# The v projection of the first stage in units of 512 channels, with tokens as the stationary side

## The chip, the cores and the metric

The kernel runs on one core of one Trainium2 chip. Its time is the device time of one execution in microseconds (us). The engines of the core are called PE (TensorE, matmuls; PEld are its weight loads), DVE (VectorE), ACT (ScalarE), POOL (GpSimd) and SP (SyncE, which issues most DMAs). Three executions of the kernel before took 2548.44, 2550.02 and 2554.36 us; the median is 2550.02 us.

## The reference

The kernel computes one layer of an encoder on 1280 tokens (1024 of a prompt, 256 of a sample) with a model width of 2048. The part that matters here is the combined input projection:

```
hn   = rmsnorm(x, norm_w)                      # 1280 x 2048
proj = einsum('btd,dp->btp', hn, w_in)         # 2048 -> 4*1024 + 5*1024 + 16 columns
na_q, na_k, na_v, na_g, ml_qk, ml_v, ml_o, ml_z, ml_gp = split(proj, ...)
```

Then neighbourhood attention uses na_q, na_k and na_v (8 heads of 128 channels), a bidirectional mLSTM uses ml_qk after a convolution, and ml_v (4 heads of 256 channels); gates, an output projection and a last rmsnorm follow. "v" below means na_v and ml_v together: 2048 columns of w_in, 16 blocks of 128 channels. All is float32; the kernel reaches the accuracy with three matmul passes over a high and a low part of both operands (high x high, high x low, low x high).

## The kernel before, in words

**Stages.** The tokens are cut in two groups. The first stage projects the first 768 tokens (GA, two halves of 384) for all columns; the second stage projects the remaining 512 tokens (among others proj_v, line 738), and attention, mLSTM and the output projection follow. Only the first stage's order is touched by the change.

**The first stage.** `pair_a` (line 479) makes two blocks of 128 channels, a "pair", at a time; a pair is named by its first block (A56 is blocks 56 and 57). The contraction over 2048 and the 768 tokens and 256 channels are each halved, and the product of the 2 x 2 blocks is made by a seven-product scheme (Strassen's, in Winograd's form): sums of quarters of x are ready in SBUF (tiles xb and xg), sums of quarters of the weights are made for each pair, and the seven products are added up into four results. The products run in the order 1, 5, 6, 4, 7, 2, 3 within each of four steps r. In each step two contraction blocks kk of 128 are done. A matmul is 128x384: the weights stand, 384 tokens move (`mm_c`, line 286, three passes). One pair has 7 x 8 x 3 = 168 of them.

**Who feeds whom.** SP loads 512 KB of weights for each r (tile ra, three buffers, line 526). POOL makes four sums of weights in each r (tile wt, line 531). ACT and DVE split every operand into a high and a low part (`split_a`, lines 184 and 185; tile wsa, eight buffers, so a split can be at most eight ahead of PE). In the last r the seven products are folded into four results: ACT copies the first (line 498), DVE adds the others from PSUM (line 494) and scales (line 263, `out_scaled`). PSUM has eight banks, three of tag "pr" and five of tag "a"; a pair takes three and four. DVE works strictly in its own order.

**What follows a pair** is a generator (`finish_a`) that the next pair advances a little after some products: for convolution pairs (blocks 24 to 39) it holds the taps (lines 424 and 430, tile cv) and stores; for q and k it splits and stores; for v pairs (from block NCH = 56) it transposes the results on PE to have tokens in rows (line 470, six couples of transposes), and `store_v` (line 233) splits and stores them: for the first four groups of 256 channels (the attention's v) two DMAs of 64 rows for each token tile (line 247), for the others one DMA (line 243). Output tiles are vo (one buffer) and pc (five buffers, shared with the results).

**The order of the work** is a list: A4, A6, then for i in 0 to 7 a convolution pair QK0 + 2i, a v pair NCH + 2i, and two other pairs. So the cycle i = 0 is A24, A56, A8, A10, and i = 1 is A26, A58, A12, A14. The sums of weights of the pairs A24, A32 and A8 to A22 are also stored for the second stage (tensor sD, line 547, by SP). A scheduler places the instructions on each engine by its own estimate of times; the code is not simply run in the order in which it is written.

## Time and profile before

| what | value |
| --- | --- |
| median of three executions | 2550.02 us |
| the profiled execution | 2548.95 us, span 2547.2 us |
| granted TensorE clock | 0.999 |
| first stage, pairs A24 to A52 | 150.15 to 1066.52 us, four pairs in some 118 us |
| one v pair without what follows it (A56) | 180.64 to 209.76 us |
| the pair behind it (A8) | 209.76 to 240.13 us |

The span runs from the first to the last instruction. A row of a list of stretches gives, for one stretch of time, how long each engine was busy, with its number of instructions in brackets, then the granted clock, the busy share of the DMA engines and GB/s. A row of the timeline gives start and length in us, engine, source line, operation, output and inputs, shape and number. In a row of one tile the three numbers are the shortest, the median and the longest duration in ns (of landings, in us from a DMA's issue).

### The profile page before, as it was taken

What the parts mean: (1) busy time and instruction counts of PE and PEld (TensorE: products, weight loads), DVE (VectorE), ACT (ScalarE), POOL (GpSimd) and SP (SyncE); (2) the same over time, 40 slices, a digit from 0 to 9 for tenths busy, and PEclk for the clock granted to TensorE, in tenths of its full rate; (3) what the DMA queues carried; (4) which work ended last, traced back from release to release, by engine and by line L of the source; (5) the groups of instructions that cost most, each with busy time, mean ns of one, the idle gap of its engine ahead of it and who ended that gap; (6) DMA issues with size and microseconds to landing.
All of it is one profiled execution on the core that took longest, in us unless ns stands there. A gap on an engine that the chain in (4) does not pass through costs nothing.

```text
span 2547.2 us, 44753 instructions
## 1 busy us (share of the span) xinstructions
PE 2527.0 (99%) x15126; PEld 2366.8 (93%) x15126; DVE 1978.3 (78%) x4040; ACT 1349.3 (53%) x3051; POOL 591.4 (23%) x894
## 2 busy tenths in 40 slices
PE   8999999999999999999999999999999999999998
PEld 8999999999999999999999899899898888888886
DVE  8768888898969798988875676776875665889695
ACT  8635545444444444475655665666665653344445
POOL 0434545444444444510000011010100103000001
PEclk9999999999999999999999999999999999999999
DMA  6556474636433343476778888888877849646227
GB/s 216 159 160 206 137 233 132 182 120 192 130 115 128 108 129 100 133 246 210 232 248 270 268 267 288 276 260 272 299 223 242 286 129 356 199 149 211 88 87 256
DMA packets 307757, 505.67 MB, mean 199 GB/s; under 512 B 48992, under 2 KB 195080, under 8 KB 307528
## 3 DMA queue, kind: packets, MB, share of 16 engines
q1 hardware_dynamic: 304568, 491.01, 60.2%
q0 software_dynamic: 2960, 11.80, 1.2%
q8 instruction: 120, 1.97, 0.3%
q14 instruction: 109, 0.89, 0.1%
HBM read 374.18 MB, written 128.52 MB: 197 GB/s over the span
## 4 chain that ended last, share of the span: by engine, by line
PE 83%; DMA 2%; DVE 1%; ACT 1%; issue 0%; SPq 0%; ACTq 0%; POOLq 0%; POOL 0%
PE po L1654 15%; PE pc L686 15%; PE pv L769 5%; PE A16b L286 1%; PE A52b L286 1%; PE A44b L286 1%; PE A40b L286 1%; PE A20b L286 1%; PE A48b L286 1%; PE A50b L286 1%; PE A42b L286 1%; PE A18b L286 1%; PE A14b L286 1%; PE A54b L286 1%; PE A70b L286 1%; PE A68b L286 1%
## 5 line engine op out<-in xcount | busy, mean ns | idle before, releaser
L1654 PE MATMUL po<-wo,mo 128*128 128x512 f32 x1620 | 375.6, 393 | 0.0
L1654 PEld LDWEIGHTS po<-wo,mo 128*128 128x128 f32 x1620 | 304.1, 188 | 70.5
L178 DVE TENSOR_TENSOR ws<-wr,ws 128x512 fp32r<-128x512 f32 x144 | 98.5, 693 | 40.0 <-ACT ws L177 39.5
L177 ACT CAST ws<-wr 128x512 fp32r<-128x512 f32 x144 | 87.6, 617 | 67.7 <-PE pc L686 55.5
L177 ACT CAST mo<-mb 128x640 fp32r<-128x640 f32 x72 | 52.0, 726 | 110.6 <-PE po L1654 100.1
L118 POOL TENSOR_SCALAR rs<-rs 128x1 f32<-128x1 f32 x10 | 4.4, 440 | 373.6 <-DVE rs L1628 373.4
L178 DVE TENSOR_TENSOR mo<-mb,mo 128x640 fp32r<-128x640 f32 x72 | 59.0, 825 | 31.3 <-ACT mo L177 31.3
L1597 DVE TENSOR_TENSOR y<-y,po 128x512 f32<-128x512 f32 x90 | 58.0, 684 | 13.2 <-PE po L1654 13.0
L177 ACT CAST mo<-ms 128x640 fp32r<-128x640 f32 x40 | 28.9, 725 | 50.7 <-PE po L1654 32.6
L178 DVE TENSOR_TENSOR wsv<-wr_v,wsv 128x512 fp32r<-128x512 f32 x64 | 44.6, 702 | 14.1 <-ACT wsv L177 13.9
L177 ACT CAST wsv<-wr_v 128x512 fp32r<-128x512 f32 x64 | 38.9, 617 | 24.5 <-PE pv L769 13.0
L424 DVE SCALAR_TENSOR_TENSOR pcv<-pco,cw_sb,pcv 128x516 f32<-128x516 f32 x48 | 36.5, 760 | 8.5 <-ACT pcv L418 8.5
L1611 ACT ACTIVATE jk<-y 128x512 f32<-128x512 f32 x40 | 25.2, 630 | 29.8 <-DVE y L1597 29.5
L178 DVE TENSOR_TENSOR mo<-ms,mo 128x640 fp32r<-128x640 f32 x40 | 32.9, 823 | 9.8 <-ACT mo L177 9.8
L131 ACT ACTIVATE xq<-xq 128x1024 f32<-128x1024 f32 x20 | 21.2, 1060 | 34.3 <-DMA xq<-in_xtok_dram 32.0
L1110 POOL MEMSET mls_0v<- 128x2 f32 x4 | 0.4, 102 | 162.5 <-DVE S_dt.float L178 137.1
L286 PE MATMUL fb<-xg,fw 128*128 128x384 f32 x192 | 34.6, 334 | 0.0
L286 PEld LDWEIGHTS fb<-xg,fw 128*128 128x128 f32 x192 | 33.4, 188 | 0.0
L807 DVE CUSTOM_DVE_ANT_0 nap_0st<-nap_0s,nap_0bt 128x384 f32<-128x384 f32 x32 | 17.7, 553 | 19.8 <-PE nap_0s L802 7.8
L1560 DVE TENSOR_TENSOR ms<-mb,mb 128x640 f32<-128x640 f32 x40 | 32.9, 823 | 0.0
L263 DVE TENSOR_TENSOR pco<-pc,rstdb 128x512 f32<-128x512 f32 x28 | 19.1, 687 | 16.7 <-PE pc L686 15.8
L810 ACT ACTIVATE nap_0st<-nap_0st,nap_0sm 128x384 f32<-128x384 f32 x32 | 19.8, 617 | 21.9 <-DVE nap_0sm L807 21.9
(2770 smaller groups left out, 8507.5 us busy)
## 6 DMA issues: line engine op xcount, KB each, us to landing
wr<-in_w_in_dram SPq DMA_DIRECT2D x72, 512.0 KB, 4.9
wr_v<-in_w_in_dram SPq DMA_DIRECT2D x32, 512.0 KB, 5.0
wb<-in_w_o_dram SPq DMA_DIRECT2D x48, 256.0 KB, 3.4
xq<-in_xtok_dram SPq DMA_DIRECT2D x20, 512.0 KB, 4.1
mb<-mx POOLq DMA_DIRECT2D x32, 320.0 KB, 7.9
y<-in_xtok_dram SPq DMA_DIRECT2D x35, 256.0 KB, 5.3
wr_wp<-in_w_o_dram SPq DMA_DIRECT2D x16, 512.0 KB, 6.5
vS<-vo SPq DMA_DIRECT2D x24, 256.0 KB, 5.2
```

Of the source, the lines that this page charges most:

```text
L131: S.activation(raw, raw, AF.Square, accum_out=ssq[g][:, t, q : q + 1])
L177: S.copy(hi, src)
L178: return V.tensor_tensor(lo, src, f(hi), op=ALU.subtract)
L286: PE.matmul(o, w(a_), x(b_), start=first and m == 0, stop=last and m == 2)
L424: V.scalar_tensor_tensor(dst[:, a:n], src[:, a + j - pad : n + j - pad], cw_sb[:, ct, j : j + 1], dst[:, a:n], op0=ALU.mult, op1=ALU.add,)
L686: PE.matmul(pb[j], t[j][:, wi, c : c + P], xs[xi], start=first and m == 0, stop=last and m == 2,)
L769: PE.matmul(outs[tt], xs[:, tt * P : (tt + 1) * P], t[:, wi, q * w : (q + 1) * w], start=first and m == 0 and (gates or tt % 2 == 0), stop ...
L810: S.activation(st, st, AF.Exp, bias=sm[:, 0:1], scale=-1.0, accum_out=sm[:, 2:3])
L1560: V.tensor_tensor(t, x, y_, op=op)
L1597: V.tensor_tensor(Y[p, q, tt], Y[p, q, tt], bk, op=op)
L1611: S.activation(jk, Y[p, q, tt], AF.Square, accum_out=ss[t][:, c : c + 1])
L1654: PE.matmul(bk[tt], m[xi][:, tt * P : (tt + 1) * P], w[wi], start=first and kk == 0 and j == 0, stop=last and j == 2, skip_group_check=True,)
```

## The change

**Units of 512 channels.** v is no longer made in eight pairs but in four units V0, V2, V4 and V6 of 512 channels (`unit_v`), which stand in the even cycles only: A24, V0, A8, A10, then A26, A12, A14, and so on. In a unit the tokens stand (slices of 128 of the tiles xb and xg) and the weights move, 256 wide, so that the result has tokens in rows at once and no transposes are needed. The seven-product scheme halves the 768 tokens (three slices of 128 each), the contraction and the 512 channels. A unit has 7 x 8 x 3 slices x 3 passes = 504 matmuls of 128x256.

**Two passes.** Seven products of 384 x 256 would take ten and a half banks of PSUM. Products 1, 5, 6, 7 and 3 are made in a first pass over the eight kk, and 2 and 4 in a second, which reads the half of the weights that it needs again. Two products share a bank for the third slice (h0, h1, h3). The first pass loads 512 KB in two DMAs for each kk, the second 512 KB in two DMAs for each r: 24 DMAs of weights in a unit, where two pairs had 8.

**Folds and stores.** ACT copies product 1, and DVE's `plus` adds the others in pieces of 512 and 256 columns. C1 and C3 are ready after the first pass, and their six token tiles are stored during the second (`finish_v`); C0 and C2 are completed by products 4 and 2 and stored during the next pair. The scaling by the norm is done in `store_v` for each token (lines 180 and 181 with a scale), no longer by `out_scaled`. The host lays the columns of v out anew, and proj_v's split follows that.

**Order on PE.** Here is the start of the first v pair, before. A56b5 is the bank of product 5, A56s05 the split operand of step 0 and product 5.

```order
L286 MATMUL A56b1_2169<-xb0_242,A56s01_2178 128x384 x3
L286 MATMUL A56b1_2169<-xb1_246,A56s01_2178 128x384 x3
L286 MATMUL A56b5_2170<-xg1_0_244,A56s05_2189 128x384 x3
L286 MATMUL A56b5_2170<-xg1_1_248,A56s05_2189 128x384 x3
L286 MATMUL A56b4_2172<-xg2_0_245,A56s04_2213 128x384 x3
L286 MATMUL A56b4_2172<-xg2_1_249,A56s04_2213 128x384 x3
```

The same place on PE after the change, in V0: V0b1 holds two slices of product 1, V0h0 the third.

```order
L481 MATMUL V0b1_2171<-V0s01_2180,xb0_242 128x256 x6
L481 MATMUL V0h0_2169<-V0s01_2180,xb0_242 128x256 x3
L481 MATMUL V0b5_2172<-V0s05_2194,xg1_0_244 128x256 x6
L481 MATMUL V0h1_2170<-V0s05_2194,xg1_0_244 128x256 x3
L481 MATMUL V0h0_2169<-V0s06_2212,xg1_0_244 128x256
L481 MATMUL V0b6_2173<-V0s06_2212,xg1_0_244 128x256 x6
```

One split operand now serves nine matmuls of 256 columns in place of six of 384, and the operands have changed sides.

**Order on DVE at the start of A8.** Before, the folds of A56 (A56c) stood there between the splits of A8 and the end of A24's convolution:

```order
L185 TENSOR_TENSOR A8s04_2552<-A8r0_2517,A8s04_2552 128x256
L185 TENSOR_TENSOR A8s07_2564<-A8t07_2561,A8s07_2564 128x256
L494 TENSOR_TENSOR A56c1_2417<-A56c0_2416,A56b7_2173 128x384
L185 TENSOR_TENSOR A8s02_2573<-A8r0_2517,A8s02_2573 128x256
L494 TENSOR_TENSOR A56c1_2417<-A56c1_2417,A56b5_2170 128x384
L494 TENSOR_TENSOR A56c0_2416<-A56c0_2416,A56b5_2170 128x384
L494 TENSOR_TENSOR A56c0_2416<-A56c0_2416,A56b2_2174 128x384
L181 SCALAR_TENSOR_TENSOR A24c1_2079<-A24cv1_2326,A24ch1_2505 128x766
L494 TENSOR_TENSOR A56c1_2417<-A56c1_2417,A56b4_2172 128x384
```

After, V0o3 and V0o5 are output tiles of V0 in the one buffer of vo, and V0c0 and V0c2 take the products of the second pass:

```order
L181 SCALAR_TENSOR_TENSOR V0o3_2858<-V0c1_2748,rstdc0_229,V0o3_2858 128x2x128
L185 TENSOR_TENSOR A8s06_3068<-A8t06_3065,A8s06_3068 128x256
L185 TENSOR_TENSOR A8s04_3077<-A8r0_3037,A8s04_3077 128x256
L185 TENSOR_TENSOR A8s07_3094<-A8t07_3091,A8s07_3094 128x256
L185 TENSOR_TENSOR A8s02_3103<-A8r0_3037,A8s02_3103 128x256
L491 TENSOR_TENSOR V0c0_2717<-V0c0_2717,V0b2_2790 128x512
L181 SCALAR_TENSOR_TENSOR V0o5_2895<-V0c1_2748,rstdc0_229,V0o5_2895 128x2x128
L185 TENSOR_TENSOR A8s03_3120<-A8t03_3117,A8s03_3120 128x256
L491 TENSOR_TENSOR V0c2_2765<-V0c2_2765,V0b4_2791 128x512
L491 TENSOR_TENSOR V0c2_2765<-V0c2_2765,V0h3_2789 128x256
```

The output V0o5 stands ahead of the fold of V0b4, and A8's product 6 is given the bank of V0b4.

**Order on DVE in an odd cycle.** Before, the convolution of A26 stood among the splits of the v pair A58:

```order
L185 TENSOR_TENSOR A58s17_3708<-A58t17_3706,A58s17_3708 128x256
L424 SCALAR_TENSOR_TENSOR A26cv0_3600<-A26c0_3480,cw_sb_961,A26cv0_3600 128x764
L185 TENSOR_TENSOR A58s12_3717<-A58r1_3656,A58s12_3717 128x256
L185 TENSOR_TENSOR A58s13_3732<-A58t13_3730,A58s13_3732 128x256
L424 SCALAR_TENSOR_TENSOR A26cv0_3600<-A26c0_3480,cw_sb_961,A26cv0_3600 128x765
```

After, it stands in the same rhythm among the splits of A12:

```order
L185 TENSOR_TENSOR A12s17_4217<-A12t17_4214,A12s17_4217 128x256
L424 SCALAR_TENSOR_TENSOR A26cv0_4103<-A26c0_3982,cw_sb_961,A26cv0_4103 128x764
L185 TENSOR_TENSOR A12s12_4226<-A12r1_4162,A12s12_4226 128x256
L185 TENSOR_TENSOR A12s13_4242<-A12t13_4239,A12s13_4242 128x256
L424 SCALAR_TENSOR_TENSOR A26cv0_4103<-A26c0_3982,cw_sb_961,A26cv0_4103 128x765
```

The convolution has moved from a v pair into a pair whose sums are also stored. Behind the first stage the order on all engines is what it was.

The diff:

```diff
--- before.py
+++ after.py
@@ -434,8 +434,6 @@
     def finish_a(n1, Cn):
         nm = f"A{n1}"
         for j in range(2):
-            if n1 >= NCH:
-                break
             if QK0 <= n1 < OT0:
                 ct = n1 - QK0 + j
                 DM.dma_start(qb[ct], Cn[j][:, GA - 4 :])
@@ -460,21 +458,119 @@
                     V.scalar_tensor_tensor(Cn[j], th, 1.0, Cn[j], op0=ALU.add, op1=ALU.mult)
                 DM.dma_start(pT[n1 + j][:, 0:GA], Cn[j])
             yield
-        if n1 >= NCH:
+    def finish_v(u, z, C):
+        for tt in range(3):
+            t = 3 * z + tt
+            if tt == 1:
+                vo = wa.tile([P, GA], F32R, tag="pc", name=f"V{u}o{t}", bufs=NPC)
+                vo = vo[:, :512].rearrange("p (a d) -> p a d", a=2)
+            else:
+                vo = wa.tile([P, 2, 256], F32R, tag="vo", name=f"V{u}o{t}", bufs=1)
+            store_v(u, t * P, vo, C[:, tt * 256 : (tt + 1) * 256], rcs[0][:, t : t + 1])
             yield
-            yield
-            yield
-            for tt in range(GA // P):
-                b = bank("a", f"{nm}v{tt}")
-                for j in range(2):
-                    PE.transpose(b[:, j * P : (j + 1) * P], Cn[j][:, tt * P : (tt + 1) * P], ident)
-                if tt in (1, 3):
-                    vo = wa.tile([P, GA], F32R, tag="pc", name=f"{nm}vo{tt}", bufs=NPC)
-                    vo = vo[:, :512].rearrange("p (a d) -> p a d", a=2)
-                else:
-                    vo = wa.tile([P, 2, 256], F32R, tag="vo", name=f"{nm}vo{tt}", bufs=1)
-                store_v((n1 - NCH) // 2, tt * P, vo, b[:, :256])
-                yield
+
+    def unit_v(u, bg):
+        nm = f"V{u}"
+        C = {}
+
+        def mm_v(b, i, kk, t, first, last):
+            for tt in range(3):
+                o = b[i][0][:, tt * 256 : (tt + 1) * 256] if tt < 2 else b[i][1]
+                own = tt == 0 or tt == 2 and b[i][2]
+                for m, (xi, wi) in enumerate(((0, 0), (0, 1), (1, 0))):
+                    PE.matmul(
+                        o, xop(i, kk, xi)[:, tt * P : (tt + 1) * P], t[:, wi],
+                        start=first and own and m == 0, stop=last and m == 2 and (tt == 1 or tt == 2 and b[i][3]),
+                    )
+
+        def parts(c, b):
+            return ((c[:, 512:], b[1]), (c[:, :512], b[0]))
+
+        def plus(q, src, bi, halves=(0, 1)):
+            for z in halves:
+                V.tensor_tensor(
+                    parts(C[q], bi)[z][0], parts(C[src], bi)[z][0], parts(C[src], bi)[z][1],
+                    op=ALU.add,
+                )
+
+        b = {}
+        h = [bank("a", f"{nm}h{j}") for j in range(2)]
+        b[1] = bank("pr", f"{nm}b1"), h[0][:, :256], True, False
+        b[5] = bank("pr", f"{nm}b5"), h[1][:, :256], True, False
+        b[6] = bank("pr", f"{nm}b6"), h[0][:, 256:], False, True
+        b[7] = bank("a", f"{nm}b7"), h[1][:, 256:], False, True
+        b[3] = bank("a", f"{nm}b3"), bank("a", f"{nm}h2")[:, :256], True, True
+        for kk in range(8):
+            r, q = divmod(kk, 2)
+            raw = wa.tile([P, 1024], F32, tag="ra", name=f"{nm}r{kk}", bufs=NRA)
+            for j in range(2):
+                DM.dma_start(
+                    raw[:, j * 512 : (j + 1) * 512].rearrange("p (f c) -> p f c", f=2),
+                    w_in[NCH // 2 + u + j, r].rearrange("p (f q c) -> p f q c", f=2, q=2)[:, :, q],
+                )
+            A = {(j, f_): raw[:, (2 * j + f_) * 256 :][:, :256] for j in range(2) for f_ in range(2)}
+
+            def summed(i, x, y_, op):
+                t = wa.tile([P, 256], F32, tag="wt", name=f"{nm}t{kk}{i}", bufs=NWT)
+                G.tensor_tensor(t, x, y_, op=op)
+                return t
+
+            src = {1: A[0, 0]}
+            for i in (1, 5, 6, 7, 3):
+                if i == 5:
+                    src[5] = summed(5, A[1, 0], A[1, 1], ALU.add)
+                elif i == 6:
+                    src[6] = summed(6, src[5], A[0, 0], ALU.subtract)
+                elif i == 7:
+                    src[7] = summed(7, A[0, 0], A[1, 0], ALU.subtract)
+                elif i == 3:
+                    src[3] = summed(3, A[0, 1], src[6], ALU.subtract)
+                t = wsa(f"{nm}s{kk}{i}")
+                split_a(t[:, 0], t[:, 1], src[i])
+                mm_v(b, i, kk, t, kk == 0, kk == 7)
+                if kk < 7:
+                    if i in (5, 7):
+                        next(bg, None)
+                    continue
+                if i == 1:
+                    for _ in bg:
+                        pass
+                    C[0] = pc(f"{nm}c0")
+                    S.copy(C[0][:, :512], b[1][0])
+                elif i == 6:
+                    S.copy(C[0][:, 512:], b[1][1])
+                    C[1] = pc(f"{nm}c1")
+                    plus(1, 0, b[6])
+                elif i == 7:
+                    C[2] = pc(f"{nm}c2")
+                    plus(2, 1, b[7])
+                    C[3] = pc(f"{nm}c3")
+                    plus(3, 2, b[5])
+                    plus(1, 1, b[5])
+                elif i == 3:
+                    plus(1, 1, b[3])
+        bg = chain(finish_v(u + 1, 1, C[3]), finish_v(u, 1, C[1]))
+        h = bank("a", f"{nm}h3")
+        b[2] = bank("pr", f"{nm}b2"), h[:, :256], True, False
+        b[4] = bank("pr", f"{nm}b4"), h[:, 256:], False, True
+        for r in range(4):
+            raw = wa.tile([P, 1024], F32, tag="ra", name=f"{nm}q{r}", bufs=NRA)
+            for j in range(2):
+                DM.dma_start(raw[:, j * 512 : (j + 1) * 512], w_in[NCH // 2 + u + j, r][:, 512:])
+            for q in range(2):
+                kk = 2 * r + q
+                for i, j in ((2, 0), (4, 1)):
+                    t = wsa(f"{nm}s{kk}{i}")
+                    split_a(t[:, 0], t[:, 1], raw[:, j * 512 + q * 256 :][:, :256])
+                    mm_v(b, i, kk, t, kk == 0, kk == 7)
+                    next(bg, None)
+                    if kk == 7:
+                        plus(j * 2, j * 2, b[i], (0, 1) if j else (1,))
+            if r == 3:
+                plus(0, 0, b[2], (0,))
+        for _ in bg:
+            pass
+        return chain(finish_v(u, 0, C[0]), finish_v(u + 1, 0, C[2]))
 
     def pair_a(n1, bg=iter(()), hook=None, first=False, pinned=False):
         nm = f"A{n1}"
@@ -615,7 +711,7 @@
     order = [4, 6]
     rest = list(range(KT0, QK0, 2)) + list(range(OT0, NCH, 2))
     for i in range(NU):
-        order += [QK0 + 2 * i, NCH + 2 * i, *rest[2 * i : 2 * i + 2]]
+        order += [QK0 + 2 * i, *((NCH + 2 * i,) if i % 2 == 0 else ()), *rest[2 * i : 2 * i + 2]]
     pools = []
 
     def second_pools():
@@ -625,7 +721,10 @@
 
     bg = opening
     for i, n1 in enumerate(order):
-        bg = pair_a(n1, bg, second_pools if i == len(order) - 1 else None, i == 0, i == 1)
+        if n1 >= NCH:
+            bg = unit_v((n1 - NCH) // 2, bg)
+        else:
+            bg = pair_a(n1, bg, second_pools if i == len(order) - 1 else None, i == 0, i == 1)
         if i == 1:
             gates_a()
         k = i - 4
@@ -746,7 +845,7 @@
             outs = [pb[t // 2][:, (t % 2) * 256 : (t % 2) * 256 + 256] for t in range(nt)]
         for r in range(4):
             raw = w_piece(w_in[NCH // 2 + u, r], f"v{u}_{r}")
-            rawv = raw.rearrange("p (j f q c) -> p f q j c", j=2, f=2, q=2)
+            rawv = raw.rearrange("p (f q c) -> p f q c", f=2, q=2)
             if gates:
                 graw = wb.tile([P, 2, 2, 16], F32, tag="wgr", name=f"wg{r}", bufs=2)
                 DM.dma_start(
@@ -755,10 +854,7 @@
             for f_ in range(2):
                 t = wb.tile([P, 2, 544], F32R, tag="wsp", name=f"wsv_{u}_{r}_{f_}", bufs=4)
                 t4 = t[:, :, : 2 * w].rearrange("p h (k c) -> p h k c", k=2)
-                h2, l2 = (
-                    t4[:, z, :, 0:256].rearrange("p q (j c) -> p q j c", j=2) for z in range(2)
-                )
-                split(h2, l2, rawv[:, f_])
+                split(t4[:, 0, :, 0:256], t4[:, 1, :, 0:256], rawv[:, f_])
                 if gates:
                     split(t4[:, 0, :, 256:272], t4[:, 1, :, 256:272], graw[:, f_])
                 for tt in range(nt):
@@ -1756,6 +1852,8 @@
     w_in = np.ascontiguousarray(
         ch.reshape(2, 4, 2, P, nb // 2, 2, P).transpose(4, 1, 3, 5, 0, 2, 6).reshape(nb // 2, 4, P, 1024)
     )
+    vw = w_in[NCH // 2 :].reshape(NU, 4, P, 2, 2, 2, P).transpose(0, 1, 2, 4, 5, 3, 6)
+    w_in[NCH // 2 :] = vw.reshape(NU, 4, P, 1024)
     gorder = [d * 8 + w_ * 4 + h for w_ in range(2) for d in range(2) for h in range(4)]
     w_g = np.ascontiguousarray(
         cols["gp"][:, gorder].reshape(KT, P, 16).transpose(1, 0, 2).reshape(P, KT * 16)
```

## The prediction

> **What bounds the kernel now.** I read the page's busy times first, then the chain that ended last, then stretches of the first stage (the only stage whose order the change touches), then the timeline inside one v pair.
>
> ```profile
> span 2547.2 us, 44753 instructions
> PE 2527.0 (99%) x15126; PEld 2366.8 (93%) x15126; DVE 1978.3 (78%) x4040; ACT 1349.3 (53%) x3051; POOL 591.4 (23%) x894
> PE 83%; DMA 2%; DVE 1%; ACT 1%; issue 0%; SPq 0%; ACTq 0%; POOLq 0%; POOL 0%
> ```
>
> PE works 99% of the span and the chain runs through it. Busy alone would not prove it, since matmul ends are modelled, so here are the stretches of one v pair (A56), the pair behind it (A8) and the next (A10), then seven stretches of three pairs each, first and sum:
>
> ```profile
> core 0: us, PE busy (x) PEld busy (x) DVE busy (x) ACT busy (x) POOL busy (x), PEclk, DMA share, GB/s
> 180.64:209.76 29.12, 29.12 (x169) 29.12 (x169) 28.83 (x46) 15.19 (x35) 15.04 (x15) 1.00 0.41 119
> 209.76:240.13 30.37, 30.37 (x179) 30.10 (x179) 24.92 (x51) 13.99 (x38) 14.45 (x18) 1.00 0.70 217
> 240.13:269.50 29.37, 29.37 (x172) 29.33 (x172) 22.86 (x46) 14.86 (x36) 15.09 (x16) 1.00 0.67 216
> ...
> 180.64:269.48 88.84, 88.84 (x518) 88.53 (x518) 76.59 (x141) 44.03 (x107) 44.59 (x48) 1.00 0.60 184
> ...
> sum 622.49, PE 622.29 PEld 620.30 DVE 540.24 ACT 301.22 POOL 301.45; mean PE 88.90 PEld 88.61 DVE 77.18 ACT 43.03 POOL 43.06
> ```
>
> The granted clock is 1.00 and in these stretches PE has no idle time. So in the first stage time is the number of matmuls times the spacing of their starts. But DVE is busy 28.83 of 29.12 us in the v pair that also carries the convolution of the pair before it: there is a second engine close behind.
>
> ```profile
> 180.64 1.20 PE L286 MATMUL A56b<-xb,A56s 128*128 128x384 f32 x6
> 181.67 6.40 PE L286 MATMUL A56b<-xg,A56s 128*128 128x384 f32 x36
> 187.91 1.20 PE L286 MATMUL A56b<-xb,A56s 128*128 128x384 f32 x6
> ...
> 208.72 1.20 PE L286 MATMUL A56b<-xg,A56s 128*128 128x384 f32 x6
> ...
> 219.12 0.38 PE L470 MATMUL A56v<-ident,A56c 128*128 128x128 f32 x2
> ```
>
> The 36 start between 181.67 and 187.91: 6.24 us, 173.3 ns each; 168 of them are the 29.12 us.
>
> **The change part by part.**
>
> Removed matmuls: eight v pairs of 168, 8 x 29.12 = 233.0 us. Removed transposes with all that they upset: the seven stretches last 622.49 us, 21 pairs at 29.12 would be 611.5; the 11.0 us over, times 8/7, is 12.5 us.
>
> Added: four units of 504 matmuls of 128x256, 2016. The nearest rows are proj_v's, the same form (tokens stationary, w_in moving, three passes); I show the row that opens a run of 27 starts and the row behind it, then matmuls with another moving operand that step faster, and twelve starts of proj_v's wider form:
>
> ```profile
> 1096.11 0.29 PE L769 MATMUL pv<-wsv,x_0l 128*128 128x272 f32 x1
> ...
> 1097.61 0.29 PE L769 MATMUL pv<-wsv,x_0l 128*128 128x272 f32 x1
> ...
> 1119.87 0.52 PE L769 MATMUL pv<-wsv,x_0h 128*128 128x256 f32 x3
> ...
> 1123.06 0.40 PE L769 MATMUL pv<-wsv,x_9h 128*128 128x256 f32 x2
> ...
> 1365.94 2.43 PE L1408 MATMUL S14by<-xs,S14s 128*128 128x256 f32 x20
> 1368.20 0.40 PE L769 MATMUL pv<-wsv,x_0h 128*128 128x256 f32 x2
> ...
> L769 PEld LDWEIGHTS pv<-wsv,x_0h x64: 187/188/192, 1095.7 to 1835.5; 128*128 128x128 f32 x64
> ```
>
> 3.19 us / 27 = 118.1 ns; the x20 give 2.26 / 20 = 113.0 ns. the wider form 1.50 / 12 = 125 ns. I take 118.1, since the new operands are of that form, and keep the other two as ends: 2016 x 0.1181 = 238.1 us (227.8 to 252.0). The stationary side is loaded anew for every matmul, and a load lasts 188 ns, more than the spacing; loads plainly overlap with work here. The Trainium skill, "TensorE: Matmul & The Clock Gate", section "The mechanism", says that weight loads overlap matmuls in flight only when the row group differs, and section "LDWEIGHTS (loading the stationary operand)" gives columns / 1.2, an estimate of 107 ns for 128; by that, an estimate, the 672 loads that are added would cost 72 us and the change would lose. All loads here use the same 128 rows, and the trace's 118.1 ns disagrees, so the sum goes by the trace.
>
> Matmuls and transposes together: 238.1 - 233.0 - 12.5 = -7.4 us. The saving is small because more, shorter matmuls cost almost what is saved.
>
> Weights are split into as many tiles as before (56 for two pairs, 56 for a unit) and summed as often (32). Three things on DVE and POOL lie closer together than before, and here PE may have to wait:
>
> ```profile
> 173.99 0.59 DVE L185 TENSOR_TENSOR A56s<-A56r,A56s 128x256 fp32r<-128x256 f32 x1 [0.56 <-ACT A56s L184]
> ...
> 184.76 0.55 DVE L263 TENSOR_TENSOR A24c<-A24c,rstdb 128x384 f32<-128x384 f32 x1
> 185.23 0.96 DVE L185 TENSOR_TENSOR A56s<-A56t,A56s 128x256 fp32r<-128x256 f32 x1
> 186.11 0.41 DVE L185 TENSOR_TENSOR A56s<-A56r,A56s 128x256 fp32r<-128x256 f32 x1
> 187.32 1.00 DVE L424 SCALAR_TENSOR_TENSOR A24cv<-A24c,cw_sb,A24cv 128x764 f32<-128x764 f32 x1
> ...
> 206.17 0.41 DVE L185 TENSOR_TENSOR A56s<-A56t,A56s 128x256 fp32r<-128x256 f32 x1
> ...
> 208.92 0.54 DVE L494 TENSOR_TENSOR A56c<-A56c,A56b 128x384 f32<-128x384 f32 x1
> ...
> 216.61 0.41 DVE L185 TENSOR_TENSOR A8s<-A8r,A8s 128x256 fp32r<-128x256 f32 x1
> ...
> 217.04 1.20 PE L286 MATMUL A8b<-xb,A8s 128*128 128x384 f32 x6
> ...
> L531 POOL TENSOR_TENSOR A56t<-A56r x8: 737/800/1440, 168.3 to 195.7; 128x256 f32<-128x256 f32 x8
> ```
>
> First pass with convolution. The first split of A56 is done at 174.58, 6.1 us before PE needs it (180.64); the last at 206.58, 2.1 us before 208.72. DVE lost 4.0 us of lead in 29.12 us. Its work there, alone: 28 splits x 0.41, ten convolution steps x 1.0, seven folds x 0.54, four scalings x 0.55 = 27.5 us; it took 33.1, so each of POOL's 16 sums cost it about 0.35 us (a split takes 0.96 instead of 0.41 when it meets one, at most 0.55). In the new unit the convolution is over after six of eight steps: 30 splits, twelve convolution steps, the same folds and scalings, 30.3 us, and 24 sums at 0.35, in all 38.7 against 30 x 9 x 0.1181 = 31.9 us of PE. The 6.8 us over meet a lead of 6.1: PE would wait 0.7 us per unit, 2.8 in four; if DVE's idle moments count for part of the 0.35, nothing. Ends 0 and, at 0.55, 5.5 us per unit. I take 0.35 per unit, 1.4 us. POOL itself has four sums per 5.3 us; at its longest, 1.44 us, they would not fit, at 0.8 easily.
>
> Start of the next pair. The unit's outputs leave through tile vo, which has one buffer; each waits for the store before it.
>
> ```profile
> L247 SPq DMA_DIRECT2D vS<-A56vo x12: 451/484/1287, 224.2 to 246.1; - x12
> L177 ACT CAST A56vo<-A56v x6: 363/372/375, 220.1 to 244.7; 128x256 fp32r<-128x256 f32 x6
> L178 DVE TENSOR_TENSOR A56vo<-A56v,A56vo x6: 409/410/425, 223.1 to 245.1; 128x256 fp32r<-128x256 f32 x6
> ...
> DMA to landing us min/median/max: 2.5/4.1/5.3
> ...
> DMA to landing us min/median/max: 2.1/2.2/2.3
> ```
>
> (The last line is A64vo's, one store per tile in place of two.) In DVE's order of the new A8, V0o5 stands ahead of the folds of V0b4, and A8's product 6 needs that bank; behind V0o5 stand A8's own splits too. From the end T of the unit's last product 6, PE has two products of the first pass, 16 of the second (18 x 1.06 us) and 25 matmuls of A8: it needs the bank at T + 23.5. DVE is done with the first output about T + 6.0 (folds of 3072 columns at 0.54 per 384, four operations of 0.41); three trips of the buffer (0.37 + 0.41 + about 1.0 for two issues + 4.1 = 5.9) end at T + 23.7, and a split (0.41) and a fold of 768 columns (1.1) follow: T + 25.2, 1.7 us late. At a landing of 2.5 us nothing is late. I take 1 us for A8 and 1 for A16. A40 and A48 have a trip of 3.3 us and no wait. The boundary of the two passes costs nothing: product 4 takes the bank whose fold is among the first after T, and PE comes there 3 us after T.
>
> Odd cycles. Units exist only in every other cycle, so the convolutions of A26, A30, A34 and A38 go into A12, A20, A44 and A52, and their lag meets folds in the pair behind. Before, that place was A8: its eighth split ended at 217.02, PE began on it at 217.04, no wait but nothing to spare. A14 and A22 have, besides, splits of q and k. Ends 0 and 1.5 us each; I take 0.75, so 1.5 us.
>
> Covered: second reading of half the weights. 8 x 512 KB in the first pass, one per 5.3 us (before: per 7.3), and 4 x 512 KB in the second, with three buffers (over 10 us ahead) against landings of 3.6 us at a DMA share of 0.41:
>
> ```profile
> L526 SPq DMA_DIRECT2D A56r<-in_w_in_dram x4: 333/358/384, 158.0 to 179.8; - x4
> ...
> DMA to landing us min/median/max: 3.6/3.6/3.7
> ```
>
> 24 issues instead of 8 on SP, 16 x 0.36 = 5.7 us more per unit of 59.5 us, ahead of stores of v that are late anyway. If pieces of 1 KB made the landing three times as long, the cover would go. ACT (15.19 of 29.12 us) loses nothing that matters.
>
> Sum: -7.4 + 1.4 + 2 + 1.5 = -2.5 us. The profiled execution took 2548.95 us (span 2547.2), so 2546.5; the median of the runs, 2550.0, is 1.1 above it: 2547.6.
>
> **Rivals.** Faster: PE never waits, and steps are shorter. No wait gives -7.4, 2542.6; at 113.0 ns, 10.3 less, 2532.3. For it: waits are small guesses; against: all L769 rows of this form step at 118.
>
> Slower, DVE against POOL in the first pass: it decides above 0.32 us of loss per sum (24 x 0.32 = 31.9 + 6.1 - 30.3), and 0.35 was worked out. At 0.45, 3.1 us per unit, 12.4 in all, 2558.6; at 0.55, 22 us, 2568. Against: DVE idles at places in A56. The Trainium skill, "SBUF — State Buffer", section "SBUF: two separate sides", says that a DVE operation with two SBUF inputs and a GpSimd operation exclude each other for a whole instruction; that is the 0.96 for 0.41 and speaks for the upper end here.
>
> Slower, stores: if v's stores land at 5.3 us, the trip is 7.1, the bank is free at T + 28.8 and A8 and A16 each wait 5.3 us: 8.6 more than the 2 taken, 2556.2. It decides from a landing of 3.5 us.
>
> Slower, loads: if weight loads of 188 ns set the step, 2016 x 0.070 = 141 us more, near 2689. Only L769 speaks against it, strongly.
>
> **Numbers.** Sum's case 0.43 (its own range 2542 to 2554), faster rival 0.17, DVE against POOL 0.21, stores 0.16, loads 0.03. Below 0.2% (5.1 us) a measurement of this kernel can't tell a change from none. Faster: 0.10 of the sum's case, 0.15 of the first rival. Slower: 0.03, 0.16 of DVE against POOL, 0.10 of stores, 0.03 of loads. Same is the rest, 0.43. The range, 2537 to 2566, leaves out the shorter steps, the uppermost part of DVE against POOL and the loads, less than 0.2.
>
> **What would show it.** In the changed trace: v matmuls at 118 ns; V0's first pass 42.5 us, second 17.0, any excess with PE waiting on A-split or V0s by DVE; a PE wait in A8 and A16 released by a V0c fold; A14 and A22 within 1 us of 29.4; no transposes. Wrong by much if one of the waits recurs at every split.

## The result and the profile after

The changed kernel takes 2554.85 us (median of 21 executions, 2552.10 to 2558.54), the kernel before 2550.84 us (21 executions beside them, 2548.44 to 2555.22). The ratio is 1.0017, 95% interval 1.0011 to 1.0023: slower by a little, 2.8 to 5.9 us. I had forecast 2547.6 us, slightly faster. The time lies within the range, but on the other side of no change. The prediction also held that below 0.2% a change can't be told from none; with 21 executions of each kernel this one, of 0.17%, can.

Busy times and the chain of the changed kernel:

```profile
span 2551.1 us, 45919 instructions
PE 2527.2 (99%) x15702; PEld 2363.9 (93%) x15702; DVE 1966.4 (77%) x4008; ACT 1343.9 (53%) x3051; POOL 608.1 (24%) x894
PE 75%; DVE 6%; DMA 3%; issue 1%; ACT 1%; SPq 0%; ACTq 0%; POOLq 0%; POOL 0%; DVEq 0%
```

PE is as busy as before, and 99% again hides the matter. The chain tells it: DVE holds 6% of it where it held 1%. DVE has less work than before (1966 against 1978 us), but part of it is late.

The span grew from 2547.2 to 2551.1 us. I take the first stage from the first matmul of A24 to the first of proj_v, first in the kernel before, then in the changed one:

```profile
150.15:1095.87 945.72, 945.52 (x5480) 943.04 (x5479) 792.02 (x1431) 454.58 (x1087) 443.64 (x506) 1.00 0.47 148
```

```profile
150.29:1098.39 948.10, 945.46 (x6056) 940.37 (x6056) 781.44 (x1398) 449.70 (x1086) 458.94 (x506) 1.00 0.48 156
```

PE's busy time didn't grow (945.5 both times), but its time without work grew from 0.2 to 2.6 us (948.10 - 945.46). As the ends of matmuls are modelled, this is less than PE really waits, as the units will show. Of the 3.9 us by which the two profiled executions differ, 2.4 lie here. The units and the pairs that got longer, in the changed kernel (V0, A8, A14, V2, A16, V4, V6):

```profile
180.78:242.01 61.23, 60.72 (x506) 59.82 (x505) 55.33 (x93) 28.52 (x68) 30.79 (x31) 1.00 0.48 150
242.01:271.47 29.46, 29.46 (x170) 29.41 (x169) 18.05 (x38) 14.01 (x39) 11.93 (x15) 1.00 0.72 210
358.85:389.17 30.32, 29.75 (x169) 29.12 (x169) 26.41 (x49) 15.41 (x37) 16.77 (x18) 1.00 0.62 218
418.30:478.83 60.53, 60.08 (x505) 59.68 (x505) 53.13 (x90) 29.45 (x70) 29.72 (x31) 1.00 0.48 149
478.83:509.29 30.46, 30.35 (x171) 29.29 (x170) 18.95 (x42) 14.02 (x39) 14.32 (x19) 1.00 0.78 232
654.92:716.15 61.23, 60.72 (x506) 59.86 (x506) 54.98 (x93) 29.22 (x70) 30.34 (x31) 1.00 0.48 156
891.21:952.45 61.24, 60.74 (x506) 59.84 (x506) 54.39 (x92) 28.70 (x69) 30.28 (x30) 1.00 0.46 156
```

A unit without any wait takes 59.59 us (an experiment below shows it), so the four units lose 1.64 + 0.94 + 1.64 + 1.65 = 5.9 us. Where, the timeline of PE in V0 shows:

```profile
211.31 0.28 PE L481 MATMUL V0b<-V0s,xg 128*128 128x256 f32 x1
211.81 0.86 PE L481 MATMUL V0b<-V0s,xg 128*128 128x256 f32 x5 [0.22 <-DVE V0s L185]
...
213.95 0.28 PE L481 MATMUL V0b<-V0s,xb 128*128 128x256 f32 x1
214.44 0.86 PE L481 MATMUL V0b<-V0s,xb 128*128 128x256 f32 x5 [0.21 <-DVE V0s L185]
```

From the matmul at 211.31 to the next pass 0.50 us where 0.12 is usual (the idle time that the view gives, 0.22, is smaller because a matmul's start and its modelled end lie 0.28 us apart). The first matmul of a split takes the high part, the second the low part, which DVE makes: what PE waits for is DVE's split (line 185). V0 has five such places, all between 202 and 215 us, where the end of the convolution of A24 lies in the unit's first pass. DVE and POOL just before the last of them:

```profile
212.01 1.49 DVE L181 SCALAR_TENSOR_TENSOR A24c<-A24cv,A24ch 128x766 f32<-128x766 f32 x1
213.43 0.95 DVE L185 TENSOR_TENSOR V0s<-V0r,V0s 128x256 fp32r<-128x256 f32 x1
...
211.84 0.86 POOL L515 TENSOR_TENSOR V0t<-V0r 128x256 f32<-128x256 f32 x1 [0.36 <-DVE V0s L185]
212.66 1.45 POOL L515 TENSOR_TENSOR V0t<-V0r,V0t 128x256 f32<-128x256 f32 x1
```

Beside POOL's sums the last step of the convolution takes 1.49 us (0.96 in the run without sums below) and the split behind it 0.95 (0.41 where it meets no sum). The split ends at 214.38, and the matmul that needs it starts at 214.44.

### The profile page after: what moved, and what is told of

Read it like the earlier page. It is cut to its first block, busy times and chain, and to the rows that moved or that the text cites. A ratio compares the mean times of both kernels' runs of the same rounds, so it can differ in the third digit from the quotient of the medians.

```text
span 2551.1 us, 45919 instructions
## 1 busy us (share of the span) xinstructions
PE 2527.2 (99%) x15702; PEld 2363.9 (93%) x15702; DVE 1966.4 (77%) x4008; ACT 1343.9 (53%) x3051; POOL 608.1 (24%) x894
## 4 chain that ended last, share of the span: by engine, by line
PE 75%; DVE 6%; DMA 3%; issue 1%; ACT 1%; SPq 0%; ACTq 0%; POOLq 0%; POOL 0%; DVEq 0%
PE pc L785 16%; PE po L1750 14%; PE pv L865 5%; PE A48b L286 1%; PE A40b L286 1%; PE A54b L286 1%; PE A52b L286 1%; PE A50b L286 1%; PE A46b L286 1%; PE A34b L286 1%; PE A42b L286 1%; PE A22b L286 1%; PE A30b L286 1%; PE A38b L286 1%; PE A44b L286 1%; PE A20b L286 1%
## 5 line engine op out<-in xcount | busy, mean ns | idle before, releaser
L481 PE MATMUL V6b<-V6s,xg 128*128 128x256 f32 x288 | 42.3, 281 | 0.2 <-DVE V6s L185 0.2
L481 PE MATMUL V4b<-V4s,xg 128*128 128x256 f32 x288 | 42.3, 281 | 0.2 <-DVE V4s L185 0.2
L481 PE MATMUL V0b<-V0s,xg 128*128 128x256 f32 x288 | 42.3, 281 | 0.2 <-DVE V0s L185 0.2
L481 PE MATMUL V2b<-V2s,xg 128*128 128x256 f32 x288 | 42.1, 281 | 0.2 <-DVE V2s L185 0.2
L481 PEld LDWEIGHTS V6b<-V6s,xg 128*128 128x128 f32 x288 | 37.5, 190 | 0.6 <-DVE V6s L185 0.4
L481 PEld LDWEIGHTS V0b<-V0s,xg 128*128 128x128 f32 x288 | 37.5, 190 | 0.6 <-DVE V0s L185 0.4
L481 PEld LDWEIGHTS V4b<-V4s,xg 128*128 128x128 f32 x288 | 37.6, 190 | 0.5 <-DVE V4s L185 0.4
```

What stands on the lines that cost most here:

```text
L481: PE.matmul(o, xop(i, kk, xi)[:, tt * P : (tt + 1) * P], t[:, wi], start=first and own and m == 0, stop=last and m == 2 and (tt == 1 or tt ...
```

## The experiments

The theory after this reading: DVE comes late because two things meet in the first pass: the convolution of the pair before, which is more work for DVE, and POOL's sums, which make DVE's operations longer. Rival A: DVE has too much work there even without POOL. Rival B: the weights come late, since they are loaded in pieces of 1 KB.

**No sums in the units.**

```diff
-                    src[5] = summed(5, A[1, 0], A[1, 1], ALU.add)
+                    src[5] = A[1, 0]
...
-                    src[3] = summed(3, A[0, 1], src[6], ALU.subtract)
+                    src[3] = A[0, 1]
```

> The unit's first pass splits raw quarters of the weights; POOL's 32 sums per unit are left out, so v is wrong in the output, but PE, ACT and the rest of DVE have the same work. Theory (POOL's sums hold DVE up while the convolution is in the first pass): V0, V2, V4 and V6 take 59.5 to 59.8 us instead of 61.2, 60.5, 61.2 and 61.2, and no PE wait stands in them. Rival A (DVE has too much work there even alone): they still take 60.5 us or more. Rival B (weights arrive late in their 1 KB pieces): no change, 61.2 us.

All four units take 59.59 us, and PE is busy for all of it (one execution; the whole kernel took 2550.38 us):

```profile
180.94:240.53 59.59, 59.59 (x506) 59.59 (x505) 45.49 (x91) 29.23 (x68) 5.58 (x7) 1.00 0.52 161
...
sum 238.36, PE 238.36 PEld 238.36 DVE 177.04 ACT 119.02 POOL 20.04; mean PE 59.59 PEld 59.59 DVE 44.26 ACT 29.75 POOL 5.01
```

That settles it against both rivals: the loads and all of the other DVE work are still there. What a sum costs can be read from DVE's groups by shape, in the stretch from V0's start to 213.5 us, first with the sums (the changed kernel), then without:

```profile
L185 DVE TENSOR_TENSOR V0s<-V0t,V0s 128x256 fp32r<-128x256 f32 x20 | 12.1, 631 | 0.0
L424 DVE SCALAR_TENSOR_TENSOR A24cv<-A24c,cw_sb,A24cv 128x766 f32<-128x766 f32 x4 | 4.5, 1126 | 0.0
L185 DVE TENSOR_TENSOR V0s<-V0r,V0s 128x256 fp32r<-128x256 f32 x5 | 3.7, 738 | 0.0
L181 DVE SCALAR_TENSOR_TENSOR A24c<-A24cv,A24ch 128x766 f32<-128x766 f32 x2 | 3.0, 1491 | 0.0
L424 DVE SCALAR_TENSOR_TENSOR A24cv<-A24c,cw_sb,A24cv 128x765 f32<-128x765 f32 x2 | 3.0, 1486 | 0.0
```

```profile
L185 DVE TENSOR_TENSOR V0s<-V0r,V0s 128x256 fp32r<-128x256 f32 x31 | 12.7, 421 | 4.2 <-ACT V0s L184 4.0
L424 DVE SCALAR_TENSOR_TENSOR A24cv<-A24c,cw_sb,A24cv 128x766 f32<-128x766 f32 x4 | 4.0, 1011 | 0.0
L424 DVE SCALAR_TENSOR_TENSOR A24cv<-A24c,cw_sb,A24cv 128x765 f32<-128x765 f32 x2 | 2.0, 1012 | 0.0
L181 DVE SCALAR_TENSOR_TENSOR A24c<-A24cv,A24ch 128x766 f32<-128x766 f32 x2 | 1.9, 958 | 0.6 <-ACT A24ch L180 0.6
```

With sums DVE never idles before a split; without them it idles 4.2 us. The same operations take longer with sums: 5.8 us in the 25 splits (20 x 0.21 + 5 x 0.32), 1.9 in the eight taps (two of them not shown), 1.1 in the two rows of line 181, and 0.6 in scalings and line 430 (not shown). That is 9.3 us, with 20 sums of POOL in the stretch: 0.47 us for each. The missing idle time also speaks against a third reading, that the sums themselves come late: DVE never waits for one here, and it is POOL that waits for DVE.

```profile
L515 POOL TENSOR_TENSOR V0t<-V0r 128x256 f32<-128x256 f32 x10 | 9.7, 975 | 9.6 <-DVE V0s L185 9.6
```

Without the sums A8 and A10 behind V0 grew by 1.2 and 0.6 us; PE waited there for ACT's split of A8 (0.71 us of it). Why that comes with the missing sums I didn't follow up.

**The unit one place later.**

```diff
-        order += [QK0 + 2 * i, *((NCH + 2 * i,) if i % 2 == 0 else ()), *rest[2 * i : 2 * i + 2]]
+        order += [QK0 + 2 * i, rest[2 * i], *((NCH + 2 * i,) if i % 2 == 0 else ()), rest[2 * i + 1]]
```

> The unit stands behind the first of the two other pairs of its cycle (A24, A8, V0, A10), so the convolution runs in A8, A16, A40 and A48. Theory and rival A: the units lose their 1.0 to 1.7 us and take 59.5 to 60.2 us (at most 1 us for folds that meet the lag in V0 and V2); the whole kernel gains 3 to 6 us on the changed one, near 2550 us. Rival B: units stay at 61.2 us and the time is that of the changed kernel.

The kernel took 2550.58 us, ratio to the kernel before 1.0002 (0.9993 to 1.0011), 4.3 us better than the changed one by the medians, as the theory has it; but its profiled first stage, 946.8 us, is only 1.3 us shorter, and where the other 3 us come from isn't shown. The units took 61.36, 61.11, 60.34 and 60.65 us, not the 60.2 or less that I had expected. The wait has moved to the start of the unit:

```profile
212.87 0.98 PE L481 MATMUL V0b<-V0s,xg 128*128 128x256 f32 x6 [0.49 <-DVE A8c L590]
...
226.83 0.84 PE L481 MATMUL V0b<-V0s,xg 128*128 128x256 f32 x5 [0.92 <-DVE V0s L185]
```

V0's third product needs a PSUM bank of A8, and its fold is late on DVE, since A8 now carries the convolution. The lag that a convolution leaves has to be worked off in the pair behind it, and a unit is a bad place for that: it takes all eight banks at once. Of the 1.3 us the units together give 0.8 (V4 and V6 got shorter, V0 and V2 longer), and the pairs 0.5: A16 is at 29.13 us, but A18 lost 0.8.

**The unit one place later, and one pair of each kind in a cycle.** In addition to the edit above:

```diff
-    rest = list(range(KT0, QK0, 2)) + list(range(OT0, NCH, 2))
+    rest = [n for z in zip(range(OT0, NCH, 2), range(KT0, QK0, 2)) for n in z]
```

> As the kernel with the unit one place later, and each cycle has one gate pair (40 to 54) and one k pair (8 to 22) in place of two of a kind: A24, A40, V0, A8, A26, A42, A10. The convolution then runs in a gate pair, which stores no sums and splits no q and k behind it. Theory: units 59.5 to 59.8 us, the waits of 1.2 us in A14 and 1.0 us in A16 go, A24 to A54 becomes 940 us instead of 948, and the kernel is 3 to 6 us faster than before the change. Rival A: same. Rival B: units at 61.2 us, and about the time of the kernel before.

```profile
210.51:271.19 60.68, 60.20 (x506) 59.99 (x506) 45.71 (x86) 27.31 (x68) 27.79 (x34) 1.00 0.49 155
...
213.40 0.97 PE L481 MATMUL V0b<-V0s,xg 128*128 128x256 f32 x6 [0.48 <-DVE A40c L590]
```

The pairs lost their waits almost wholly, as expected (A14 29.13, A16 29.13 us). The units did not: 60.67, 60.67, 60.77 and 60.43 us, a wait of about 0.75 us in each for the late fold of the pair ahead, and 0.33 us more in three of them from a slower spacing of matmuls (last section). The first stage took 943.8 us, and the kernel 2551.72 us, ratio 1.0007 (0.9998 to 1.0016): no gain over the kernel before. The part from proj_v on took 1455.3 us here; I come back to that.

**The unit last in its cycle.** The lag has a whole pair to go before the unit begins:

```diff
-    rest = list(range(KT0, QK0, 2)) + list(range(OT0, NCH, 2))
+    rest = [40, 8, 42, 10, 44, 12, 46, 14, 48, 16, 50, 18, 20, 22, 52, 54]
...
-        order += [QK0 + 2 * i, *((NCH + 2 * i,) if i % 2 == 0 else ()), *rest[2 * i : 2 * i + 2]]
+        order += [QK0 + 2 * i, *rest[2 * i : 2 * i + 2], *((NCH + 2 * i,) if i % 2 == 0 else ())]
```

> Each unit stands last in its cycle, behind a k pair, so that two pairs lie between a convolution and a unit: A24, A40, A8, V0, A26, A42, A10, A28 and so on; the seventh cycle is A36, A20, A22, V6 and the eighth A38, A52, A54 as before the change. Theory (a unit waits only where DVE comes into it late, by convolution and sums together or by the folds behind a lagging pair): V0, V2 and V4 take 59.6 us with no PE wait, V6 at most 60.8; one wait of about 1.2 us is left in A22; A24 to A54 takes 940 to 942 us (945.7 before the change, 948.1 with it); the kernel is 2 to 6 us faster than before the change. Rival (a unit makes waits of its own wherever it stands): V0, V2 and V4 at 60.3 us or more, and no gain over the kernel before.

```profile
PE 95%; DVE 2%; DMA 2%; ACT 0%; SPq 0%; issue 0%; ACTq 0%; POOLq 0%; POOL 0%; DVEq 0%
```

```profile
238.45:298.04 59.59, 59.59 (x505) 59.59 (x505) 43.65 (x84) 28.07 (x68) 28.91 (x31) 1.00 0.48 154
...
sum 238.34, PE 238.34 PEld 238.34 DVE 173.30 ACT 107.30 POOL 108.83; mean PE 59.59 PEld 59.59 DVE 43.33 ACT 26.83 POOL 27.21
...
149.71:1090.08 940.37, 940.37 (x6056) 939.78 (x6055) 784.09 (x1397) 448.06 (x1085) 455.85 (x506) 1.00 0.48 157
```

The kernel takes 2544.53 us (11 executions, 2543.05 to 2547.94), ratio to the kernel before 0.9978 (0.9969 to 0.9987). It beats both kernels, by 5.6 and by about 10 us. All units stand at 59.59 us, sums included, and the chain is PE's for 95%. The first stage lasts 940.37 us, 5.35 less than before the change. The 5.35 us are near the 6.9 that matmuls and transposes give (below). The wait of 1.2 us that I expected in A22 did not come (29.13 us); why is said below. The kernel before was not run in this order, so what the order alone would do for it isn't shown.

**Another end of the list.**

```diff
-    rest = [40, 8, 42, 10, 44, 12, 46, 14, 48, 16, 50, 18, 20, 22, 52, 54]
+    rest = [40, 8, 42, 10, 44, 12, 46, 14, 48, 16, 50, 18, 52, 20, 22, 54]
```

> As the kernel before it, but the seventh cycle is A36, A52, A20, V6 and the eighth A38, A22, A54: the convolution of A38 runs in a k pair at the very end. Theory: no wait in V6 or in A20; one of 1.0 to 1.3 us in A54, as in A14 of the changed kernel; the same first stage within 1 us. If the end of the first stage decides what the second one loses, the part from the first proj_v matmul on is 1 us or more longer than in the kernel with A52 and A54 last.

2544.31 us, ratio 0.9977 (0.9968 to 0.9987): the same. The first stage is 940.3 us, no wait in A54 (29.13 us), and the part from proj_v on 1452.8 us against 1452.4. My expectation of a wait in A54 failed like that for A22, and for the same reason.

**Is the part behind the first stage slower?** In the two profiled executions it was 1.3 us longer with the change (1452.7 against 1451.3), though the order of instructions there is the same. One suspect is the new layout of v's columns, which proj_v reads. The kernel before with the layout alone:

```diff
+    vw = w_in[NCH // 2 :].reshape(NU, 4, P, 2, 2, 2, P).transpose(0, 1, 2, 4, 5, 3, 6)
+    w_in[NCH // 2 :] = vw.reshape(NU, 4, P, 1024)
...
+            if n1 >= NCH:
+                rv = raw.rearrange("p (f q j c) -> p j f q c", f=2, q=2, j=2)
+                A = {(j, f_): rv[:, j, f_] for j in range(2) for f_ in range(2)}
```

> The kernel before with only the new host layout of v's columns and proj_v's contiguous split; the first stage reads the quarters with a stride. Theory (the changed kernel's 1.3 us behind the first stage are scatter): span from the first proj_v matmul to the end 1451 to 1453 us, time within 1.5 us of the kernel before. Rival (the layout costs the second stage its 1.3 us): that part takes 1452.5 us or more and the kernel is 1.3 us or more slower.

2550.43 us, ratio 0.9997 (0.9988 to 1.0006), and 1451.2 us from proj_v on. No cost of the layout shows, and the interval leaves room for 1.5 us at most. Then both kernels twice more:

> The kernel before, once more, to see how much the part behind the first stage varies from execution to execution. If the 1.3 us that the changed kernel has there are scatter, this part takes 1451.3 us give or take 1.5 us; if they belong to the change, within 0.5 us of 1451.3.

> The changed kernel, once more. Scatter: the part behind the first stage anywhere from 1450.5 to 1454 us. A cost of the change: 1452.2 to 1453.2 us. The first stage repeats in both cases, with units of 60.5 to 61.3 us.

> As the first repetition of the kernel before: scatter gives a spread of 1 us or more between the repetitions behind the first stage, a cost of the change gives less than 0.5 us.

> As the first repetition of the changed kernel: scatter gives 1450.5 to 1454 us behind the first stage, a cost of the change 1452.2 to 1453.2 us.

The part behind the first stage took 1453.0 and 1456.1 us in the kernel before, 1453.0 and 1453.2 us in the changed one. With the two first executions, before: 1451.3 to 1456.1; after: 1452.7 to 1453.2. It is scatter, larger than the difference that it was to explain and wider than the 1.5 us that I had allowed. The first stage repeats: 945.7, 946.4 and 945.8 us before; 948.1, 949.4 and 949.0 us after, a difference of 2.9 us on the mean. That is what the change costs in these profiles, and it lies at the lower end of the interval of the ratio. Whether v2's 1455.3 us belong to its order, where A22 comes last, or to the scatter, stays open.

## Why the prediction was right or wrong

**Added and removed matmuls: right.** Worked out: -7.4 us. Measured: -6.9. The 2016 matmuls of four units without a wait take 4 x 59.59 = 238.4 us for my 238.1; 118.2 ns each, for the 118.1 taken from proj_v. That it is so close is partly luck, as 118.2 is the mean of three different spacings (last section). The rival of shorter steps fell, and weight loads are hidden here as in proj_v: one lasts 188 ns, and matmuls start 118 ns apart. The Trainium skill's sentence in "TensorE: Matmul & The Clock Gate" ("The mechanism") that loads overlap only when the row group differs is not borne out by these units either.

**First pass with convolution: the step that failed.** The mechanism was right, its size was not. I took 0.35 us of wait per unit, 1.4 us in all; it is 1.47 on the mean, 5.9 in all. The working gave 0.7 per unit with a loss of 0.35 us for each sum, and I then halved it, on the thought that DVE's idle moments in A56 were counted in.

The halving went the wrong way. Compared row by row with rows that meet no sum, a sum costs 0.47 us in V0 (above), and in A56 too some 0.45: the rows of that stretch add up to 34.7 us, not 33.1, against the 27.5 without sums, for 16 sums. My subtraction missed this because rows of DVE that follow each other overlap by about 0.08 us (two splits in a row take 0.75 us, not 0.82); that hid more than the 1.3 us for which DVE was idle there.

The threshold that I had named, 0.32 us, was passed, so the mechanism of the slower rival "DVE against POOL" is what happened. Its price was not: put into my sum, 0.47 gives 30.3 + 24 x 0.47 - 31.9 - 6.1 = 3.6 us per unit, over twice the 1.6 of three units. A sum of rows leaves out their overlaps, some 4 us for its 53 operations, so it can't be right to a microsecond, and that 0.7 and 1.47 are of one order is luck.

What the traces show directly is the lead, from the end of DVE's split to the first matmul that uses the tile. In the first pass of V0 it falls, in the changed kernel, from 6.0 us to below zero at five of the splits 21 to 31, the five places where PE waits; without the sums it stays above 4.4 us, and with the unit last above 2.5.

A split that meets a sum takes 0.96 us in place of 0.41, so 0.55 more, while the sums beside the convolution last 0.85 to 1.45. The Trainium skill, "SBUF — State Buffer", section "SBUF: two separate sides", has a DVE operation with two SBUF inputs and a GpSimd operation exclude each other for a whole instruction; the runs agree that sums hold DVE up, and show that on the mean a sum costs DVE 0.47 us, less than the sum's length. Whether an operation that begins during a sum is shut out until its end can't be read from these means.

**Start of the next pair: right in size by luck, wrong in kind.** I took 1 us each for A8 and A16. They lost 0.34 and 1.33 us, but not at the bank. In A8 the store landed soon enough:

```profile
243.60 0.48 DVE L181 SCALAR_TENSOR_TENSOR V0o<-V0c,rstdc,V0o 128x256 fp32r<-128x256 f32 x1 [2.09 <-ACT V0o L180]
...
244.94 0.75 DVE L491 TENSOR_TENSOR V0c<-V0c,V0h 128x256 f32<-128x256 f32 x2
...
DMA to landing us min/median/max: 2.2/2.8/4.3
```

DVE does stand still for 2.09 us before V0o5, as I had read from its order, but the folds are done at about 245.7 us, and PE comes for the bank only at about 246.4 (242.01 and 25 matmuls). The landings are 2.8 us, not 4.1. A8's 0.34 us are slower steps (below), and so are the 0.30 each in A40 and A48, for which I had taken nothing. A16 lost about 1.0 us in its third and fourth step r, where splits came late: in the third, ACT waited 2.52 us for a load of the other tokens' x (tile xq) and squared it before it could go on to the splits; in the fourth, it waited 3.06 us for a store of v. The first of these is on no line of my sum.

**Odd cycles: A14 longer than I took, A22 misread.** A14 took 30.32 us, 1.2 too long, for 0.75 taken; A22 had nothing, for 0.75. The chain that I gave, lag of a convolution, then folds, then splits of q and k, accounts for about half of what A14 lost. In A22 it can't apply, since I had wrongly counted A16 to A22 among the k pairs. The kernel splits results for q and k only below block 16 (GT0), and blocks 16 to 23 are na_g. Of the pairs that carry a convolution in odd cycles only A12 is a k pair. PE in A14, then what DVE has to do there for the results of A12, and in A22 for those of A20:

```profile
362.62 4.29 PE L286 MATMUL A14b<-xg,A14s 128*128 128x384 f32 x23 [0.31 <-DVE A12c L590]
...
374.85 0.97 PE L286 MATMUL A14b<-xb,A14s 128*128 128x384 f32 x4 [0.26 <-DVE A14s L185]
...
370.42 2.17 DVE L178 TENSOR_TENSOR A12s_dt.float<-A12c,A12s_dt.float32r 128x512 f32<-128x512 f32 x2
...
372.85 1.61 DVE L178 TENSOR_TENSOR A12s_dt.float<-A12c,A12s_dt.float32r 128x512 f32<-128x512 f32 x2
...
607.56 2.36 DVE L458 SCALAR_TENSOR_TENSOR A20c<-A20th,A20c 128x768 f32<-128x768 f32 x2
```

The second wait of A14, about half of its 1.2 us, comes right behind these splits of k. The first, for a fold of A12, begins earlier, in A12:

```profile
342.57 1.06 ACT L131 ACTIVATE xq<-xq 128x1024 f32<-128x1024 f32 x1 [2.83 <-DMA xq<-in_xtok_dram]
...
344.05 0.42 DVE L185 TENSOR_TENSOR A12s<-A12r,A12s 128x256 fp32r<-128x256 f32 x1 [0.61 <-ACT A12s L184]
```

ACT waited for a load of xq, so its split and then DVE's came late. Up to there DVE's rows stand in A12 where they stand in A20, counted from the pair's start; from there on they come 0.69 us later, up to the fold for which PE waits. This is read from one trace; no run was made without these squares or without the splits of k. It also explains the two expectations that failed, a wait in A22 with the unit last and one in A54 in the order behind it: the pairs ahead, A20 and A22, hold na_g, so no splits of k follow.

**Covered parts: right.** The second reading of weights, the boundary of the two passes, ACT and the 24 issues on SP cost nothing that the trace shows: units without sums, and units behind a pair that is caught up, run at 59.59 us with all of these in place.

In sum, the first stage: -6.9 us for matmuls and transposes (238.4 added, 233.0 and 12.3 removed, the latter being what the pairs behind the eight v pairs took above 29.13 us), +5.9 for waits within units, +3.4 for the pairs behind units and in odd cycles (A8, A14, A16, A40, A48; 3.5 taken): 2.4 us, as measured. The term that turned the result is the first pass: it was 4.5 us too small, more than the whole forecast gain. That 3.4 stands against 3.5 is luck, since A8, A14, A16, A22, A40 and A48 were each off, and in part for reasons that my sum didn't have.

## What to carry to other kernels

A change that saves a few us on a bound engine lives or dies by the lead of the engine behind it: write that lead down at the start and the end of each stretch (6.1 and 2.1 us in A56), and don't take a discount on a term that has passed its own threshold. Look up in the kernel which pairs do which work, rather than count them by their numbers. If a second engine's backlog is the trouble, moving the new work two places away from what makes the backlog can be worth more than the change: the same units went from 61.2 to 59.59 us by order alone. One place away was not enough, as the lag was only passed on.

## What the runs showed of the hardware

The same form of matmul, 128x256, ran at three steady spacings in one unit: in V0, nine in 1.06 us at the start (180.78 to 181.84, 117.8 ns each), nine in 1.08 us in the later part of the first pass (206.62 to 207.70, 120 ns), and nine in 1.02 us (113.3 ns) in the first half of the second pass. The units without waits have the same three:

```profile
228.27 0.84 PE L481 MATMUL V0b<-V0s,xg 128*128 128x256 f32 x6
228.95 0.50 PE L481 MATMUL V0h<-V0s,xg 128*128 128x256 f32 x3
229.29 0.84 PE L481 MATMUL V0b<-V0s,xg 128*128 128x256 f32 x6
```

The pair behind a unit carries on with such a state: A8's first half steps at 176.8 ns (36 in 6.36 us), its second half at 173.3, at a granted clock of 1.00 and with no wait:

```profile
243.08 6.52 PE L286 MATMUL A8b<-xg,A8s 128*128 128x384 f32 x36
249.44 1.22 PE L286 MATMUL A8b<-xb,A8s 128*128 128x384 f32 x6
...
257.92 6.40 PE L286 MATMUL A8b<-xg,A8s 128*128 128x384 f32 x36
264.16 1.20 PE L286 MATMUL A8b<-xb,A8s 128*128 128x384 f32 x6
```

In the order with the unit one place later and the kinds mixed, three units ran the first half of their second pass at 117.8 ns instead of 113.3, and the pairs behind them at 173.3 at once. What sets the spacing was not tried; with 113.3 ns throughout, the 2016 matmuls would, by an estimate from these figures, take 10 us less.
